# Row maxima of a 64 MB tensor: another split of the loads, and 48 blocks instead of 36 on GpSimd, 22 of them read out by a diagonal selection and summing copies

## The chip, the cores and the metric

The kernel runs on one core of a Trainium2 chip. The metric is the device time of one execution in microseconds (us), the median of several runs. One further execution is taken with the hardware profiler; its rows are what this document reads.

## What is computed

```python
x = np.random.randn(32, 512, 1024).astype(np.float32)
out = np.max(x, axis=-1)          # (32, 512), float32
```

16384 rows of 1024 numbers; each row gives its maximum. All 67.1 MB are read once from HBM.

## The kernel before

**Tiling.** The 16384 rows are laid over 128 partitions, 128 rows for each. A *load* of n rows brings n whole rows to every partition (n x 4 KB each, n x 512 KB in all) by one DMA on SyncE's (SP's) queue. `BLOCKS` lists the sizes: 17 loads, of 2, 16, 14, 15, 13, 12, 10, 9, 8, 7, 6, 4, 3, 2, 2, 1 and 1 rows, numbered from 0. The last three rows come in six *pieces* of 384 to 640 columns (`PIECES`: row, width). The data lands in `ring`, which has room for 47 rows a partition: loads take places in order and start again from the front when the next doesn't fit. A load is issued (`issue`, L263 to L276) when the program has passed the last reader of the place it overwrites; on the chip SP then waits for that reader's semaphore. Each of eight semaphores serves every eighth transfer, so a transfer also waits until the one eight before it has landed.

**VectorE** reduces whole rows: `direct` (L215, steps d) takes the rows of one load in one `reduce_max` (every reduction is recorded at L76, the helper `maximum`). For a piece (steps f) it reduces the piece together with one column in front of it, in which the maximum of the row's earlier piece lies.

**GpSimd's share.** `SHARED` maps a load to (rows, blocks of 128 columns of each such row, rows per chunk, ...): these blocks go another way, 36 of the 1024 in this kernel, in chunks of 3 or 6 blocks. For a chunk k:

- t: TensorE transposes its 128x128 blocks into PSUM (`turn`, L148; L155)
- c: ScalarE copies them to SBUF, tile `sb` (`fetch`, L162; L166)
- r: GpSimd takes the maximum over the 128 partitions, `partition_all_reduce`, into `top` (`across`, L169; L173); every partition then holds all the results
- b: TensorE turns row 0 of `top` back, one 1x128 transpose a block, into `small` (`back`, L177; L184)
- e: ScalarE copies these columns beside the rest of the row's partial maxima (`keep`, L192; L194)

The other columns of such rows are reduced by VectorE (`partial`, L221, steps p), and a last small reduction joins both (`merge`, L228, steps m). The loads in `RANK` write into one tile `joint` and share one merge, m99, at the very end; load 10 has tile `parts` and m10. `select` (L196, steps s) and `sums` (L204, steps x) are in the kernel's text, but its plan doesn't call them.

**Order.** `PLAN` (L30) writes out the order of all steps by hand; `in_turn` chains the instructions of each engine in that order, so every engine is one queue in which an instruction that waits holds up all behind it. The tiles `ps`, `sb` and `top` have two buffers each: chunk k waits until chunk k-2 has been read. The results of the first 116 rows a partition are stored behind the first f step, those of the last 12 after m99, both from ScalarE's queue (L301, L303).

Of the kernel before, what the change touches and what calls it, by code (L numbers as in the profile page):

```python
# [10 lines left out]


BLOCKS = [
    [2, 16, 14, 15, 13, 12, 10, 9, 8, 7, 6, 4],
    [3, 2, 2, 1, 1],
]
RING = 47

SHARED = {10: (6, 3, 2, 0), 12: (3, 3, 2, 0), 14: (2, 3, 1, 0), 16: (1, 3, 2, 0)}


RANK = {12: 1, 14: 2, 16: 2}


PIECES = [(2, 640), (0, 576), (1, 512), (1, 512), (0, 448), (2, 384)]


PLAN = """  # L30
    d0 d1 d2 d3 d4 d5 d6 d7 d8 d9 t0 p10 t1 c0 r0 t2 c1 d11 r1 c2 b0 e0 r2 b1 e1 t3 p12 t4
    c3 b2 c4 r3 d13 e2 r4 m10 t5 p14 b3 c5 t6 r5 d15 e3 b4 c6 t7 p16 e4 r6 b5 f0 c7 e5 f1 r7
    b6 f2 e6 f3 b7 f4 e7 f5 m99
""".split()

NOSYNC = mybir.DependencyInfo(mybir.DependencyClass.NoSync, mybir.DependencyReason.DATA)
# [4 lines left out]
def kernel(  # L41
# [33 lines left out]
    def maximum(out, in_):  # L75
        return in_turn("DVE", nc.vector.reduce_max(out=out, in_=in_, axis=X))  # L76
# [17 lines left out]
    views = []  # L94
    last = 1 + max(r for r, _ in PIECES)
    first = at = 0
    for sizes in BLOCKS:
# [6 lines left out]
        b, place = 0, {}  # L104
        for i in sorted(range(len(sizes)), key=lambda i: RANK.get(base + i, 0)):
            place[i] = b
# [8 lines left out]
    assert first == I  # L115
    shared = [SHARED.get(j, (0, C, 1, 0)) for j in range(len(loads))]

    lead = [n - s[0] for (_, n, _, _), s in zip(loads, shared)]
    final = [j for j in range(len(loads)) if j in RANK]
    final.sort(key=lambda j: loads[j][3])  # L120
# [10 lines left out]
    def rows(j):  # L131
        start, n, _, _ = loads[j]
        return ring[:, I + start * D:I + (start + n) * D].rearrange("p (i d) -> p i d", d=D)
# [5 lines left out]
    def share(j):  # L139
        m, parts, _, _ = shared[j]  # L140
        if j in RANK:
            r = loads[j][3] + lead[j] - col0
            return joint[:, r:r + m, :]
        if j not in fetched:
            fetched[j] = once.tile([P, m, parts + (parts < C)], F32, name=f"parts{j}")
        return fetched[j]
# [74 lines left out]
    def partial(j):  # L221
        m, parts = shared[j][:2]

        s = width - parts if j in RANK else 1
        maximum(share(j)[:, :, parts:], rows(j)[:, lead[j]:lead[j] + m, parts * P:].rearrange(
# [14 lines left out]
    before = [None] * last  # L240
    for r, w in PIECES:
        c, q = done[r], before[r]
# [90 lines left out]
```

## Time and profile before

| | |
|---|---|
| median of 3 runs | 163.65 us (163.60 to 163.66) |
| the profiled execution | 163.59 us, of it 161.8 us from the first to the last instruction (span) |
| mean DMA rate over the span | 415 GB/s (67.11 MB read) |
| VectorE (DVE) busy | 135.5 us, 84% of the span |
| GpSimd (POOL) busy | 15.9 us, 8 all-reduces from 141.3 us on |
| TensorE (PE) | 13.3 us; ScalarE (ACT) 7.3 us |

How to read it: a row of a group names the line, the engine, the operation, the tiles written and read, the count, and then the busy time, the mean duration of one in ns, and the idle time of the engine ahead of it with what ended it. Rows in order of time give the start and the length in us. SPq and ACTq are the queues of SP and ScalarE that issue DMAs. An instruction often starts some 0.08 to 0.1 us before the one ahead of it in its engine has ended, so durations add up to a little more than the time they take.

### The profile page before, as it was taken

What the parts mean: (1) busy time and instruction counts of PE and PEld (TensorE: products, weight loads), DVE (VectorE), ACT (ScalarE), POOL (GpSimd) and SP (SyncE); (2) the same over time, 40 slices, a digit from 0 to 9 for tenths busy, and PEclk for the clock granted to TensorE, in tenths of its full rate; (3) what the DMA queues carried; (4) which work ended last, traced back from release to release, by engine and by line L of the source; (5) the groups of instructions that cost most, each with busy time, mean ns of one, the idle gap of its engine ahead of it and who ended that gap; (6) DMA issues with size and microseconds to landing.
All of it is one profiled execution on the core that took longest, in us unless ns stands there. A gap on an engine that the chain in (4) does not pass through costs nothing.

```text
span 161.8 us, 304 instructions
## 1 busy us (share of the span) xinstructions
PE 13.3 (8%) x72; PEld 11.1 (7%) x72; DVE 135.5 (84%) x33; ACT 7.3 (5%) x17; POOL 15.9 (10%) x13
## 2 busy tenths in 40 slices
PE   0000000000000000000000000000000000647471
PEld 0000000000000000000000000000000000637350
DVE  3500009999999929999999999999999999999994
ACT  0020000000000000000000000000000000142230
POOL 0000000000000000000000000000000000097991
PEclk9999999999999999999999999999999999995555
DMA  5996998799999599999988997999999899999991
GB/s 198 579 486 292 518 472 383 312 454 454 486 486 486 243 454 421 421 448 561 401 389 389 486 466 344 437 437 421 478 429 439 376 475 395 433 410 412 408 389 38
DMA packets 3600, 67.18 MB, mean 415 GB/s; under 512 B 656, under 2 KB 912, under 8 KB 1680
## 3 DMA queue, kind: packets, MB, share of 16 engines
q1 hardware_dynamic: 3312, 67.11, 97.0%
q10 hardware_dynamic: 288, 0.07, 0.2%
HBM read 67.11 MB, written 0.07 MB: 415 GB/s over the span
## 4 chain that ended last, share of the span: by engine, by line
DVE 63%; DMA 35%; issue 0%; SPq 0%; DVEq 0%
DVE ring L76 58%; DMA ring<-in_x_dram 35%; DVE parts L76 3%; DVE joint L76 2%; SPq L270 0%; DVEq L328 0%; DVEq L76 0%
## 5 line engine op out<-in xcount | busy, mean ns | idle before, releaser
L76 DVE TENSOR_REDUCE ring<-ring 128x2 f32<-128x2048 f32 (+17 forms) x19 | 125.7, 6660 | 23.0 <-DMA ring<-in_x_dram 22.9
L173 POOL PARTITION_ALL_REDUCE top<-sb x8 | 15.6, 2013 | 134.9 <-ACT sb L166 134.5
L155 PE MATMUL ps<-ident,ring 128*128 128x128 f32 x36 | 8.9, 426 | 141.1 <-DMA ring<-in_x_dram 141.0
L155 PEld LDWEIGHTS ps<-ident,ring 128*128 128x128 f32 x36 | 7.0, 222 | 141.2 <-issue 141.2
L166 ACT COPY sb<-ps 128x768 f32<-128x768 f32 (+1 forms) x8 | 5.0, 640 | 139.1 <-PE ps L155 137.7
L184 PE MATMUL small<-ident,top 1*128 1x1 f32 x36 | 4.8, 238 | 4.4 <-POOL top L173 4.4
L184 PEld LDWEIGHTS small<-ident,top 1*128 1x128 f32 x36 | 4.1, 197 | 6.4 <-POOL top L173 5.0
L76 DVE TENSOR_REDUCE joint<-ring 128x3 f32<-128x1920 f32 (+2 forms) x3 | 4.4, 1483 | 0.0
L76 DVE TENSOR_REDUCE parts<-ring 128x6 f32<-128x3840 f32 x1 | 4.1, 4144 | 0.0
L166 ACT ACT_TABLE_LOAD x1 | 1.3, 1283 | 7.7 <-DVE ring L76 7.7
L194 ACT COPY joint<-small 128x3 f32<-128x3 f32 (+1 forms) x5 | 0.8, 164 | 2.3 <-PE small L184 2.3
L81 DVE MEMSET ident<- 128x128 f32 x1 | 0.2, 165 | 0.8 <-PEq L317 0.8
L288 POOL MEMSET gate<- 128x1 f32 x1 | 0.1, 100 | 7.3 <-DVE ring L76 7.3
L194 ACT COPY parts<-small 128x6 f32<-128x6 f32 x3 | 0.5, 166 | 2.6 <-PE small L184 2.5
L88 DVE TENSOR_SCALAR rowno<-rowno 32x1 f32<-32x1 f32 x3 | 0.4, 147 | 0.1
L83 DVE TENSOR_TENSOR_SCAN colno<-ident 128x128 f32<-128x128 f32 x1 | 0.4, 424 | 0.0
L90 DVE TENSOR_SCALAR ident<-colno,rowno 128x128 f32<-128x128 f32 x1 | 0.3, 286 | 0.0
L85 DVE STREAM_TRANSPOSE rowno<-colno 128x32 f32<-128x32 f32 x1 | 0.2, 211 | 0.0
L76 DVE TENSOR_REDUCE ring<-joint 128x6 f32<-128x24 f32 x1 | 0.2, 169 | 0.0
L76 DVE TENSOR_REDUCE ring<-parts 128x6 f32<-128x24 f32 x1 | 0.2, 168 | 0.0
L317 POOL MEMSET const-float32-0.0<- 128x1 f32 x1 | 0.1, 100 | 0.2 <-issue 0.2
L317 POOL MEMSET const-bfloat16-1.0<- 128x1 bf16 x1 | 0.1, 102 | 0.0
(3 smaller groups left out, 0.3 us busy)
## 6 DMA issues: line engine op xcount, KB each, us to landing
ring<-in_x_dram SPq DMA_DIRECT2D x1, 7680.0 KB, 57.6
ring<-in_x_dram SPq DMA_DIRECT2D x1, 7168.0 KB, 40.0
ring<-in_x_dram SPq DMA_DIRECT2D x1, 6656.0 KB, 33.6
ring<-in_x_dram SPq DMA_DIRECT2D x1, 6144.0 KB, 33.1
ring<-in_x_dram SPq DMA_DIRECT2D x1, 5120.0 KB, 26.2
ring<-in_x_dram SPq DMA_DIRECT2D x1, 4608.0 KB, 36.7
ring<-in_x_dram SPq DMA_DIRECT2D x1, 4096.0 KB, 32.9
ring<-in_x_dram SPq DMA_DIRECT2D x1, 3584.0 KB, 28.2
```

Of the source, the lines that this page charges most:

```text
L76: return in_turn("DVE", nc.vector.reduce_max(out=out, in_=in_, axis=X))
L81: in_turn("DVE", nc.vector.memset(ident, 1.0))
L83: in_turn("DVE", nc.vector.tensor_tensor_scan(out=colno, data0=ident, data1=ident, initial=-1.0, op0=ALU.add, op1=ALU.mult))
L85: in_turn("DVE", nc.vector.transpose(out=rowno, in_=colno[:, :32]))
L88: in_turn("DVE", nc.vector.tensor_scalar(out=part, in0=part, scalar1=float(q * 32), scalar2=None, op0=ALU.add))
L90: in_turn("DVE", nc.vector.tensor_scalar(out=ident, in0=colno, scalar1=rowno[:, 0:1], scalar2=None, op0=ALU.is_equal))
L155: in_turn("PE", nc.tensor.transpose(out=ps[:, w:w + P], in_=rows(j)[:, lead[j] + r + i, c * P:(c + 1) * P], identity=ident,))
L166: in_turn("ACT", nc.scalar.copy(out=sb[:, :W], in_=filled[k][:, :W]))
L173: in_turn("POOL", nc.gpsimd.partition_all_reduce(top[:, :W], turns[k][:, :W], P, bass_isa.ReduceOp.max))
L184: in_turn("PE", nc.tensor.transpose(out=small[:, i, c:c + 1], in_=tops[k][0:1, w:w + P], identity=ident[0:1, 0:1],))
L194: in_turn("ACT", nc.scalar.copy(out=share(j)[:, r:r + q, :shared[j][1]], in_=smalls[k]))
L317: nc = _bacc.Bacc("TRN2", target_bir_lowering=False, num_devices=1)
```

## The change

It changes the tables and the plan; the functions stay. The loads become 2, 15, 14, 16, 14, 13, 11, 10, 9, 7, 5, 3, 2, 2, 1, 1 and 1 rows, with four pieces for two rows. GpSimd's share grows to 48 blocks in ten chunks, from loads 8, 9, 10, 11, 13, 14 and 16; chunks have 6, 4, 6, 6, 8, 4, 6, 4, 2 and 2 blocks. Chunks 0 to 3 (22 blocks) are read out without TensorE: `select` on GpSimd sets to zero, in each 128x128 block of `top`, all but the diagonal, so that partition p keeps the maximum of row p, and `sums` on ScalarE adds up the 128 columns of each block with an accumulating copy, which leaves that maximum. The other chunks go through b and e as before. Four merges take the place of two: m8, m9, m10, m99.

```diff
 BLOCKS = [
-    [2, 16, 14, 15, 13, 12, 10, 9, 8, 7, 6, 4],
-    [3, 2, 2, 1, 1],
+    [2, 15, 14, 16, 14, 13, 11, 10, 9, 7, 5],
+    [3, 2, 2, 1, 1, 1],
 ]
-SHARED = {10: (6, 3, 2, 0), 12: (3, 3, 2, 0), 14: (2, 3, 1, 0), 16: (1, 3, 2, 0)}
-RANK = {12: 1, 14: 2, 16: 2}
-PIECES = [(2, 640), (0, 576), (1, 512), (1, 512), (0, 448), (2, 384)]
+SHARED = {8: (5, 2, 3, 1), 9: (4, 3, 2, 1), 10: (3, 4, 2, 0), 11: (3, 2, 4, 0), 13: (2, 2, 4, 0), 14: (1, 2, 1, 0), 16: (1, 2, 3, 0)}
+RANK = {11: 1, 13: 2, 14: 2, 16: 2}
+PIECES = [(0, 576), (1, 576), (0, 448), (1, 448)]
 PLAN = """
-    d0 d1 d2 d3 d4 d5 d6 d7 d8 d9 t0 p10 t1 c0 r0 t2 c1 d11 r1 c2 b0 e0 r2 b1 e1 t3 p12 t4
-    c3 b2 c4 r3 d13 e2 r4 m10 t5 p14 b3 c5 t6 r5 d15 e3 b4 c6 t7 p16 e4 r6 b5 f0 c7 e5 f1 r7
-    b6 f2 e6 f3 b7 f4 e7 f5 m99
+    d0 d1 d2 d3 d4 d5 d6 d7 t0 d8 t1 c0 c1 r0 p8 s0 r1 x0 s1 x1 t2 d9 t3 c2 r2 c3 m8 p9 s2
+    r3 x2 t4 d10 t5 c4 p10 s3 c5 r4 x3 t6 p11 m9 d12 r5 c6 b4 e4 r6 b5 p13 t7 e5 t8 c7 m10
+    p14 r7 c8 b6 d15 e6 p16 t9 r8 b7 c9 f0 e7 r9 b8 f1 e8 f2 b9 f3 e9 m99
 """.split()
```

The two functions that the plan newly calls (unchanged):

```python
def select(k):
    j, _, q = chunks[k]
    B = q * shared[j][1]
    view = tops[k][:, :B * P].rearrange("p (b w) -> p b w", w=P)
    in_turn("POOL", nc.gpsimd.affine_select(
        out=view, in_=view, pattern=[[0, B], [-1, P]], compare_op=ALU.is_equal,
        fill=0.0, base=0, channel_multiplier=1))

def sums(k):
    ...
    in_turn("ACT", nc.scalar.activation(
        out=tops[k][:, w:w + P], in_=tops[k][:, w:w + P],
        func=mybir.ActivationFunctionType.Copy,
        accum_out=share(j)[:, r + i, c:c + 1]))
```

## The prediction

> **What bounds the kernel now.** I read the slices first, then the stages (busy time, DMA share and GB/s in stretches that I set), then the chain of waits, then the tail in order of time. From the page:
>
> ```profile
> DMA  5996998799999599999988997999999899999991
> q1 hardware_dynamic: 3312, 67.11, 97.0%
> ```
>
> The dips of the DMA row are packets of 56 to 64 KB booked in the slice where they end; the stages even them out (us and length, PE, PEld, DVE, ACT, POOL busy, PE clock, DMA share, GB/s):
>
> ```profile
> 2.00:138.50 136.50, 0.00 (x0) 0.00 (x0) 113.52 (x13) 1.28 (x1) 0.10 (x1) 1.00 1.00 433
> 138.50:153.50 15.00, 9.50 (x52) 8.26 (x53) 15.00 (x7) 4.23 (x9) 11.23 (x5) 0.76 0.99 415
> 153.50:158.50 5.00, 3.49 (x21) 2.63 (x20) 4.93 (x8) 1.64 (x7) 4.40 (x4) 0.50 0.93 346
> ```
>
> From 2 us until about 158.5 the 16 DMA engines never rest. VectorE idles early (113.5 of 136.5 us busy) and is full only from 90 us. The chain of waits shows the one stretch of it that hides this:
>
> ```profile
> 56.91 33.10 DMA ring<-in_x_dram
> 90.00 0.02 issue
> 90.03 49.46 DVE ring L76 x5
> ```
>
> The chain puts 49 us on VectorE, but it starts when a load landed, and in the end VectorE only just keeps up with the loads: the last piece is issued at 153.44 us and takes 5.3 us to land, so 158.7, and its reduction starts at 158.87. In the order of time:
>
> ```profile
> 155.56 3.86 DVE L76 TENSOR_REDUCE ring<-ring 128x1 f32<-128x640 f32 x6
> 158.85 0.16 ACT L194 COPY joint<-small 128x3 f32<-128x3 f32 x1 [1.25 <-PE small L184]
> 159.33 0.17 DVE L76 TENSOR_REDUCE ring<-joint 128x6 f32<-128x24 f32 x1
> 159.53 0.34 ACTq L303 DMA_DIRECT2D out_dram<-ring  x1
> ```
>
> Two things meet at the final merge (m99, 159.33): the last piece's reduction, and GpSimd's last result, which lay ready at 159.02, 0.3 us early. **Both bounds count:** the load stream by a hair, GpSimd's chain close behind.
>
> **The load stream.** From the landings in the trace (5.32, 24.64, 41.58, 59.73, 75.47, 90.00, ... us) a load of n rows a partition costs 1.2045 n + 0.075 us; pieces cost 1.2045 us a row plus about 0.07 each (they land at 155.54, 156.30, 156.97, 157.65, 158.25, 158.72). The bytes stay, 17 loads stay 17, two pieces go: 2 x 0.07 = 0.14 us less. Laid out with the new sizes the landings are 105.7 (11 rows), 117.9 (10), 128.8 (9), 137.3 (7), 143.4 (5), 147.1 (3), 149.6, 152.05, 153.3, 154.6, 155.9, and pieces at 156.6, 157.4, 158.0, 158.57. The ring still gives room in time: load 4 (14) goes out when the 15 rows are reduced (39.6 us, with data queued until 59.7), load 8 (9) at 106.4 (queued until 117.9), load 10 (5) at 118.2 (queued until 137.3). SP's pieces wait only for the landing eight transfers earlier, the last for 149.6; it is needed at 158. So the stream does not stall.
>
> **VectorE.** A reduction costs 1.0415 ns an element plus 0.06 net (10.809 us for 10240, 4.419 for 4096, each starting 0.083 before the one ahead ends). It gives 12 more blocks away, 12 x 0.133 = 1.6 us, and gets 27 reductions for 24, +0.2: 1.4 us less work. None of it shortens the end, since it already waits for landings: laid row by row, it starts d9 at 137.3, d10 at 143.4, p13 at 152.06, p16 at 155.90, each as its load lands, and f3 (449 elements, 0.61 us, where the last was 385, 0.54) at 158.62; m99 follows at 159.15 and ends at 159.32. The same layout of the old plan gives 159.37 (the trace has 159.50). Difference: **-0.05 us**. Behind it nothing changes: the store's issue, its landing and the end take 2.3 us.
>
> **GpSimd.** Its rows:
>
> ```profile
> L173 POOL PARTITION_ALL_REDUCE top<-sb x4 | 10.0, 2543 | 134.5 <-ACT sb L166 134.5
> L173 POOL PARTITION_ALL_REDUCE top<-sb x4 | 5.7, 1483 | 0.4 <-PE small L184 0.4
> ```
>
> The first (140 to 150 us) are four of 768 columns, the second (from 152.3) four of 384. Back to back they start 2.486 and 1.407 us apart: 0.33 us + 2.81 ns a column, so 1.77 for 512, 3.21 for 1024, 1.05 for 256. The ten new ones sum to 20.5 us (15.6 before); the diagonal selections of 768, 512, 768 and 768 columns come on top, and no row shows one. **Bounds:** from below, GpSimd's memset of one element, 0.1 us; from above, the all-reduce of the same tile, 2.5 us, which also crosses partitions. The nearest row is an elementwise comparison, VectorE's is_equal on 128 columns, 0.286 us; at its 1.04 ns a column 768 would take 0.95. I take 1.0 us (0.7 for 512), on GpSimd an estimate.
>
> **The sums** are 22 small ScalarE passes with an accumulator, also in no row. ScalarE's copies: 800 ns for 768 columns and 479 for 384, so 0.16 + 0.00084 a column; 0.27 for 128, less the 0.10 by which neighbours overlap: 0.16 from below. From above, no overlap and a second small instruction (0.164): 0.43. I take 0.30. Gone are 22 of TensorE's 48 one-row transposes and four of ScalarE's small copies, both off the path; TensorE's 12 added transposes, 0.213 each, lie in its gaps (the largest group, t4, ends at 145.5, and c4 behind x2 starts at 145.57).
>
> Laid in the order written out: load 8 lands at 128.8; before, the first all-reduce began 2.7 us behind its landing (138.57 to 141.25), so r0 at 131.4, s0 133.98, r1 134.98, s1 136.8 to 137.5, sums x1 until 138.8. ScalarE's copy c2 stands behind x1 and needs load 9 (137.3 + 1.75): 139.05, so r2 starts at 139.9 and GpSimd rests 2.4 us. Then r2 2.5, s2 1.0, r3 2.5, s3 1.0 until 147.03; r4 needs c4, which stands behind x2 on ScalarE: ready 146.67, so 0.36 early. r4 to r9 then run without rest: 150.2, 151.9, 154.35, 156.1, 157.1 and, since r9 waits for the buffer of r7 to be read, 158.33. One transpose and one copy later, 159.0, its maxima are there; VectorE wants them at 159.15. Merges m8, m9 and m10 find their parts 1.7, 0.7 and 0.9 us early. **So the cover is about 0.15 us at the end, 0.3 with the pause before r9**, thinner than the trace's own 0.3; it is gone when a selection of 768 passes 1.2 us, or a sum 0.36.
>
> **Sum against the profiled 163.59:** 163.54; the median of the runs is 0.06 above it: **163.6 us**, no change. A measurement of this kernel can tell about 0.2% (0.33 us) from none.
>
> **Rivals.**
> A. *The selection is slow*, slower. GpSimd's only long row has 2.81 ns a column, so 1 ns is a hope. All four count, 3.3 times the excess, because s0 and s1 push c2 as s2 and s3 push r4: at 1.35 us +0.55, at 1.7 (midway of 0.95 and 2.5) +1.85, so 165.5; at 2.5, +4.8. It decides from 1.2 us. The Trainium skill's "GPSIMD Engine Reference" (3.1) speaks for it: even a tight one-input loop takes about 1.8 cycles an element at 1.2 GHz, two-input work 2.6; 768 columns would be estimated at 1.15 to 1.66 us, and the sum at 163.6 to 165.3. No run here shows which. Against A stands only that the other engines' elementwise rows lie near 1 ns a column.
> B. *The sums are slow and block ScalarE's queue*, slower: behind x2 wait c4 and so r4, behind x3 c6 and so r6. At 0.43 each +0.6 us, 164.2; with a selection of 1.35 as well, +1.6. For it: an accumulator that must be read out. Against: the 0.10 overlap in the rows.
> C. *VectorE is the bound*, faster, as the chain's 63% has it: the 1.4 us would count, 162.2. Against it: the DMA share of 1.00 and the reductions that start as loads land.
> That the change does not do what it says I rule out: the built order has 48 blocks, four selections, 22 sums and four pieces.
>
> **Chances.** Forecast 0.53; A 0.24 (mostly 1.3 to 1.8 us, 164 to 165.6); B 0.16 (164 to 165.2); C 0.07. So faster 0.07, same 0.53, slower 0.40. The forecast's own range is 163.4 to 163.9. The range runs to 165.4, which leaves out C and the dear third of A; the bounds of 2.5 and 0.43 together (+5.5, 169) lie beyond and hold some 0.04.
>
> **What would show it.** Right: the stages still show a DMA share of 1.00 until 158 us, the last piece is reduced near 158.6, m99 starts at once behind it, selections near 1.0 and sums near 0.30. A: selection rows over 1.2, m99 idle behind ScalarE's copy, no rest on GpSimd between s1 and r9. B: copies L166 idle-free behind L210, r4 waiting for ScalarE. C: the last piece landing before 157.5. I would be wrong altogether if a load were issued too late and the DMA share fell before 150 us.

## The result and the profile after

The changed kernel takes **164.09 us** (median of 9 runs, 164.00 to 164.38) against 163.66 (9 runs, 163.55 to 163.93): ratio 1.0026, 95% interval 1.0016 to 1.0037. It is slower by 0.43 us; 163.6 was forecast. The profiled execution, the slowest of the nine, took 164.38, of it 162.7 us span.

The page of the changed kernel, DMA row and queues (packets, MB, share of the 16 engines):

```profile
DMA  5999699999799979999999998989999899999990
...
q1 hardware_dynamic: 3024, 67.11, 96.4%
q10 hardware_dynamic: 288, 0.07, 0.2%
q14 instruction: 1, 0.01, 0.0%
```

The last row is new: one packet of instructions, 8 KB, while the kernel runs. The page of before has no such row. The stages, as in the prediction (PE, PEld, DVE, ACT, POOL busy, PE clock, DMA share, GB/s):

```profile
2.00:138.50 136.50, 3.15 (x14) 2.81 (x15) 112.05 (x14) 5.48 (x22) 5.86 (x5) 1.00 1.00 432
138.50:152.70 14.20, 7.33 (x41) 6.08 (x40) 14.20 (x9) 8.00 (x33) 12.33 (x7) 0.71 0.99 415
152.70:158.50 5.80, 3.80 (x20) 2.62 (x20) 5.58 (x7) 1.98 (x7) 5.17 (x4) 0.50 0.96 367
158.50:159.20 0.70, 0.12 (x1) 0.12 (x2) 0.70 (x2) 0.00 (x0) 0.53 (x1) 0.50 0.01 5
```

The DMA engines are as full as before, and the bytes are the same. VectorE is less busy than before (112.05 us for 113.52 until 138.5). The tail of VectorE in order of time:

```profile
152.38 1.76 DVE L76 TENSOR_REDUCE joint<-ring 128x2 f32<-128x1536 f32 x1
154.05 0.16 DVE L76 TENSOR_REDUCE ring<-parts 128x3 f32<-128x15 f32 x1
154.12 0.94 DVE L76 TENSOR_REDUCE joint<-ring 128x1 f32<-128x768 f32 x1
155.23 1.22 DVE L76 TENSOR_REDUCE ring<-ring 128x1 f32<-128x1024 f32 x1 [0.17 <-DMA ring<-in_x_dram]
156.51 0.95 DVE L76 TENSOR_REDUCE joint<-ring 128x1 f32<-128x768 f32 x1
157.38 2.46 DVE L76 TENSOR_REDUCE ring<-ring 128x1 f32<-128x576 f32 x4
159.76 0.17 DVE L76 TENSOR_REDUCE ring<-joint 128x7 f32<-128x21 f32 x1
```

m99 starts at 159.76 (before: 159.33), and VectorE waits for a load ahead of 155.23. The chain of waits ends in the loads as well:

```profile
129.07 0.02 issue
129.09 27.39 DMA ring<-in_x_dram
156.49 0.02 issue
156.51 0.95 DVE joint L76
```

So the stream of loads is late. A load is done when all 16 engines have landed their part. The trace's landings, first and last of the 16, in us:

```
                        changed            before           (one copy, below)
load 13, 2 rows      151.88  152.36                          151.81  152.19
load 14, 1 row       153.20  154.09     151.82  152.15 *     153.10  153.48
last piece           158.40  159.13     158.41  158.72       158.35  158.70
* load 14 of before has 2 rows and lies elsewhere in the stream
```

Between loads 13 and 14 the gap from first to last landing grows from 0.48 to 0.89 us, and it is still 0.72 at the end. With one copy it goes from 0.38 to 0.35 over the same loads, so some 0.27 us of the step is left at the last piece. At load 14 one engine lands 0.46 us behind the fifteenth. The first engine ends as early as before (158.40, 158.41); the load is done when the late one is. The packets of that time show why:

```
q14  8192 bytes  at 152.78 us, 313 ns
q1   4096 bytes  at 153.10 us, 319 ns     (usual: 160 ns)
q1   4096 bytes  at 153.40 us, 379 ns
```

A window around it has the packet in the profile's own view:

```profile
q1 hardware_dynamic: 63, 0.20, 102.7%
q14 instruction: 1, 0.01, 3.9%
```

It comes when ScalarE stands at its 63rd row of 81 (before has 34 rows in all). The profiled run of the changed kernel has slower packets of 56 to 64 KB at 11 to 47 us too; by load 13 it is 0.17 us behind the run with one copy (152.36, 152.19). Such packets come up in another profiled run (before_16_copies, below) whose median time is that of before, so they are taken as this run's own. And it loses 0.3 us behind m99: its last store is issued at 160.01 and lands at 161.78, after 1.77 us (before 1.41, with one copy 1.46). Of the 0.79 us between the two profiled executions only the 0.43 at m99 can so be put down to the loads; what the fetch costs in the median is read from the experiments.

### The profile page after: what moved, and what is told of

Same layout as the page of the kernel before. It is cut to its first block, busy times and chain, and to the rows that moved or that the text cites. A ratio compares the mean times of both kernels' runs of the same rounds, so it can differ in the third digit from the quotient of the medians.

```text
span 162.7 us, 367 instructions
## 1 busy us (share of the span) xinstructions
PE 14.6 (9%) x74; PEld 11.8 (7%) x74; DVE 134.3 (83%) x36; ACT 15.6 (10%) x61; POOL 24.1 (15%) x19
## 4 chain that ended last, share of the span: by engine, by line
DMA 77%; DVE 20%; SPq 0%; issue 0%; DVEq 0%
DMA ring<-in_x_dram 77%; DVE ring L76 19%; DVE joint L76 1%; SPq L270 0%; DVEq L328 0%
## 5 line engine op out<-in xcount | busy, mean ns | idle before, releaser
L76 DVE TENSOR_REDUCE ring<-ring 128x2 f32<-128x2048 f32 (+11 forms) x17 | 118.2, 6987 | 24.6 <-DMA ring<-in_x_dram 24.6
L173 POOL PARTITION_ALL_REDUCE top<-sb x10 | 20.6, 2093 | 127.1 <-ACT sb L166 126.4
L155 PE MATMUL ps<-ident,ring 128*128 128x128 f32 x48 | 11.3, 408 | 141.7 <-DMA ring<-in_x_dram 138.4
L155 PEld LDWEIGHTS ps<-ident,ring 128*128 128x128 f32 x48 | 8.7, 211 | 143.2 <-issue 133.6
L166 ACT COPY sb<-ps 128x768 f32<-128x768 f32 (+3 forms) x10 | 6.6, 669 | 127.1 <-PE ps L155 124.1
L76 DVE TENSOR_REDUCE parts<-ring 128x5 f32<-128x3840 f32 (+2 forms) x3 | 8.7, 2899 | 0.0
L210 ACT ACTIVATE top<-top 128x128 f32<-128x128 f32 x22 | 6.5, 296 | 6.0 <-POOL top L200 6.0
L76 DVE TENSOR_REDUCE joint<-ring 128x1 f32<-128x768 f32 (+2 forms) x4 | 6.2, 1549 | 0.1
L210 ACT ACTIVATION_READ_ACCUMULATOR top<-top 128x1 f32 x22 | 4.1, 186 | 0.0
L200 POOL TENSOR_SCALAR_AFFINE_SELECT top<-top 128x768 f32<-128x768 f32 (+1 forms) x4 | 3.2, 806 | 0.3
```

The lines of the kernel that those rows point to most:

```text
L155: in_turn("PE", nc.tensor.transpose(out=ps[:, w:w + P], in_=rows(j)[:, lead[j] + r + i, c * P:(c + 1) * P], identity=ident,))
L166: in_turn("ACT", nc.scalar.copy(out=sb[:, :W], in_=filled[k][:, :W]))
L173: in_turn("POOL", nc.gpsimd.partition_all_reduce(top[:, :W], turns[k][:, :W], P, bass_isa.ReduceOp.max))
L200: in_turn("POOL", nc.gpsimd.affine_select(out=view, in_=view, pattern=[[0, B], [-1, P]], compare_op=ALU.is_equal, fill=0.0, base=0, channe ...
L210: in_turn("ACT", nc.scalar.activation(out=tops[k][:, w:w + P], in_=tops[k][:, w:w + P], func=mybir.ActivationFunctionType.Copy, accum_out= ...
```

## The experiments

Theory F: the added ScalarE rows (22 accumulating passes are 44 rows, a pass and a read of the accumulator each) take ScalarE's queue past a block of instructions; fetching the next block takes one DMA engine out of a stream that never rests. Rivals: G, GpSimd's chain ends last; L, the new split of the loads is slower; R, ScalarE's added work at the end holds up what stands behind it. All are against runs of the kernel before on the same chip.

**1. after_one_copy.** In `sums`, one copy a chunk, which leaves the summing out (the removed lines are shortened here):

```diff
-        for i in range(q): for c in range(parts): nc.scalar.activation(..., accum_out=...)
+        in_turn("ACT", nc.scalar.copy(out=share(j)[:, r:r + q, :parts], in_=view[:, :, :, 0]))
```

> The changed kernel, but the 22 accumulating passes are replaced by four copies, one a chunk, that take column 0 of each block; what lands in the partial maxima of loads 8 and 9 is then not the row's maximum, so this kernel leaves the summing out. ScalarE has 4 rows in place of 44 there. Theory F (an 8 KB transfer of instructions on queue q14 at 152.8 us, seen only in the changed kernel, holds up one of the 16 DMA engines, and the last loads wait for that engine): the transfer is gone, the spread between the first and the last of a load's 16 landings stays near 0.3 to 0.5 us to the end (0.89 at load 14 in the changed kernel), and the time is 0.4 to 0.5 us below the changed kernel's 164.09, so 163.6 to 163.7. Rival G (GpSimd's chain is what ends last, since the final copy before m99 lay ready only 0.1 us early): GpSimd's rows are the same, the time stays within 0.15 us of 164.09. Rival L (the new split of the loads makes the stream slower, as packets of 56 to 64 KB took up to 0.28 us longer at 11 to 47 us): 164.09 stays as well, with the fetch gone.

Measured: 163.67 us; ratio to before 1.0000 (0.9991 to 1.0009). No q14 row, the spread 0.35 to 0.40 us from the first load to the last piece. GpSimd's ten all-reduces and four selections and the new loads are all there, so G and L as they were meant fall: with the fetch gone the slowdown is gone.

**2. before_44_copies, 3. before_16_copies.** To the kernel before, behind d0, in ScalarE's idle time:

```diff
+                for _ in range(44):        # 16 in the other
+                    in_turn("ACT", nc.scalar.copy(out=idle[:, 0:1], in_=ident[:, 0:1]))
```

> The kernel before with 44 copies of one column on ScalarE at about 8 us, where it has nothing to do for 130 us: as many more instructions on ScalarE as the sums brought (78 rows in place of 34). Theory F: ScalarE's queue now needs one more block of instructions, an 8 KB packet on q14 appears near the ScalarE row that is the 62nd (about 154 us), one engine falls behind by 0.4 us, and the time is 0.2 to 0.5 us above before (163.85 to 164.15). Rivals G and L: no difference, 163.66 within 0.1.

> The same with 16 copies, 50 rows on ScalarE. Theory F, if a count between 50 and 81 brings the transfer: no packet on q14 after the start, 163.66 within 0.1. If any added instruction cost time here (against F), it would lie between before and the run with 44.

Measured: 44 copies 164.01 us, ratio 1.0016 (1.0007 to 1.0025), with a q14 packet at 157.97; 16 copies 163.69, ratio 1.0000 (0.9991 to 1.0009), no packet. Work of 10 us in a hole of 130 us costs 0.3 us when it has enough rows, and nothing when it has not. But the profiled run with 44 copies, which took 163.86, less than the median, doesn't show F's path: the packet came too late to widen the spread of the last landings (0.54 at load 1, 0.45 at the last piece). It shows another delay. Behind its semaphore at 154.89 us ScalarE starts its 64th row, a copy, only 0.38 us later, where the same copy takes 0.06 us with 16 copies. GpSimd's last result then lies ready 0.07 us ahead of m99 (0.32 with 16 copies), and the last store goes out 0.28 us behind the start of m99 (0.20). So extra rows may also cost a pause of the engine itself; whether this pause belongs to the next block of instructions, and how much of the 0.3 us it makes, isn't shown. With 120 copies, below, rows 50 to 78 have no such pause.

**4. after_ten_sums.** Chunks 2 and 3 through steps b and e, and without s and x, in the plan.

> The changed kernel with chunks 2 and 3 read out by transposes and copies (steps b and e) as before, so 10 blocks instead of 22 go by selection and sums, two selections of 0.86 us and 24 rows of ScalarE less. The result is whole. Theory F: about 59 rows on ScalarE; if that stays under the count, no transfer in the middle and 163.55 to 163.7, below both kernels or level with before; if the transfer still comes, it comes later than 152.8 us and costs up to 0.4. Rival G: GpSimd has 1.7 us less to do, so 0.1 to 0.2 us less than 164.09 with or without the transfer. Rival L: 164.0 to 164.1.

Measured: 163.82 us, ratio to before 1.0010 (1.0001 to 1.0019): no q14 row with 58 rows on ScalarE, and the load stream ends at 158.66. Less than the changed kernel, as F has it, though 0.1 above what was expected and not better than before.

**5. before_120_copies, 6. after_60_more.** The same copies, 120 in the kernel before and 60 in the changed one, to bring the fetch forward.

> The kernel before with 120 copies of one column on ScalarE from 9 us on (0.22 us each, so until 36 us; ScalarE has nothing else before 140 us). Theory F, with a transfer of 8 KB of instructions each time ScalarE has gone through some 63 to 69 rows: a packet on q14 near 23 us, perhaps a second at the end. If the engine that carries it stays behind until the last load (the load queue never runs empty, so nothing lets it catch up), the time is 0.2 to 0.5 us above before as with the late transfer: 163.9 to 164.15. If it catches up, 163.7 within 0.1. Rival R (ScalarE's work at the end, not the transfer, cost the time in the changed kernel): no difference, 163.69.

> The changed kernel with 60 copies of one column on ScalarE from 9 to 23 us. Theory F: the transfer of 152.8 us comes at about 23 us instead, and no load of the end shows a new lag; the time stays at 164.0 to 164.2 if the lag is carried to the end, and falls to 163.6 to 163.7 if it is caught up or if only a late transfer costs. A second transfer at the end (141 rows in all) would add up to 0.4.

Measured (before: 163.90 on this chip): 164.26, ratio 1.0024 (1.0015 to 1.0033), packet at 24.13 us; 164.28, ratio 1.0025 (1.0016 to 1.0034), packet at 23.28 us, none at the end. The 1.0025 is the 1.0026 of the changed kernel. The fetch now falls 135 us from the end, and it costs as much: the late engine has hardly caught up. In after_60_more the spread is 0.41 us for the first load, 1.13 and 0.97 for the next two, 0.97 still at 158.31 and 0.89 at the last piece. The profile of the 120 copies can't show this. Its first load is already 0.75 us apart, before the copies begin, and the engine that carries the fetch is 0.63 us ahead of the slowest (their packets end at 24.13 and 24.76 us), which hides the 0.60 us that it loses; so this run's cost stands on its median alone.

R falls with the profile of the changed kernel: r4 starts at 147.06, with one copy, so without the sums, at 146.91, and these 0.15 us are what the loads are behind by then. GpSimd also rests 0.6 us before its last all-reduce, which waits for TensorE and so for load 16; a delay from the sums would have been taken up there.

```profile
POOL top L173 <- PE small L184: 0.6, 1, 0.6
```

**7. before_60_gpsimd, 8. before_60_vector.** 60 memsets of one element, on GpSimd in the same place, and on VectorE behind d0.

```diff
+                for _ in range(60):
+                    in_turn("POOL", nc.gpsimd.memset(gate[:, 1:2], 0.0))     # or "DVE", nc.vector.memset(idle[:, 0:1], 0.0)
```

> The kernel before with 60 memsets of one element on GpSimd at about 8 us (92 rows in place of 32), where it has nothing to do until 141 us. Theory F, if every engine fetches by its own count: a packet on q14 in the middle, +0.2 to +0.5 us. If the transfer belongs to ScalarE alone: no packet, 163.69 within 0.1.

> The same with 60 memsets of one element on VectorE behind its first reduction, in the 17 us in which it waits for the load of 16 rows (101 rows in place of 41). Theory F for every engine: a packet on q14, late, since VectorE's 62nd row then lies about 8 us in or, counted from the second block, near the end; +0.2 to +0.5 us. ScalarE alone: no packet, 163.69 within 0.1.

Measured: GpSimd 164.18, ratio 1.0019 (1.0010 to 1.0028), packet at 19.40 us, at GpSimd's 71st row; VectorE 164.60, ratio 1.0039 (1.0027 to 1.0052), packet at 17.08 us, at its 71st row. From the rows of the run with the memsets on VectorE, the memsets and then the page's queues:

```profile
L292 DVE MEMSET idle<- 128x1 f32 x60 | 3.5, 59 | 3.9
```

```profile
q1 hardware_dynamic: 3312, 67.11, 96.5%
q10 hardware_dynamic: 288, 0.07, 0.2%
q14 instruction: 1, 0.01, 0.0%
```

3.5 us of memsets in a wait of 17 us, and the kernel is 0.7 us longer. So each of the three engines fetches by its own count. What the carrying engine lost (fetch and excess in ns, their sum in us), and how the spread of the landings moved (us):

```
                    fetch   next packets' excess    sum     spread before, after
changed kernel        313   159 + 219              0.69     0.48 -> 0.89
after_60_more         309   293                    0.60     0.41 -> 0.97
before_60_gpsimd      309   254                    0.56     0.37 -> 0.77
before_60_vector      309   562                    0.87     0.34 -> 1.20
```

Where the carrier was not already the slowest of the 16, part of its loss is hidden. In the last three rows it was 0.11, 0.29 and 0.11 us ahead of the slowest when the fetch came, and the ends of the next packets spread 0.49, 0.27 and 0.76 us wider than those before: the sum less this lead. The landings spread by some 0.1 us more again, for which no run gives a cause.

**9. one_copy_select_twice, 10. ten_sums_smaller_end.** In the plan of the first experiment `s3 s3` for `s3`; in after_ten_sums `PIECES = [(0, 640), (1, 640), (0, 384), (1, 384)]`.

> The kernel with one copy a chunk instead of the sums (63.67 above 100, no transfer of instructions; what it leaves out is told there), with the last of the four selections done twice, which adds 0.86 us to GpSimd's chain and changes nothing in the data. If GpSimd's chain has the thin cover that the prediction gave it (0.15 us at the merge and 0.3 at the pause before r9), the merge comes 0.3 to 0.5 us later and the time is 0.3 to 0.5 us above the kernel before: 164.0 to 164.2. If GpSimd is hidden by more than that, no difference, within 0.1 of before. If every microsecond of GpSimd counts, +0.86.

> The changed kernel with ten sums (no transfer of instructions), with pieces of 640, 640, 384 and 384 columns for 576, 576, 448 and 448, so that the last reduction has 384 columns and one more: 0.07 us less behind the last landing. Nothing else changes. Theory F with a stream that is the only other bound: 0 to 0.1 us below after_ten_sums, level with the kernel before (within 0.2 us), and no version of this plan gains more, since the bytes are the same. If VectorE's 1.4 us of relief counted anywhere, it would show as 0.5 us or more below before.

(The "63.67 above 100" is 163.67.) Measured: 164.27, ratio to before 1.0039 (1.0025 to 1.0052), above the range expected; and 163.76, ratio 1.0006 (0.9997 to 1.0015). The end of the first, in order of time:

```profile
159.63 0.16 ACT L194 COPY joint<-small 128x2 f32<-128x2 f32 x1 [0.89 <-PE small L184]
159.69 0.38 ACTq L296 DMA_DIRECT2D out_dram<-ring  x1
159.83 0.17 DVE L76 TENSOR_REDUCE ring<-joint 128x7 f32<-128x21 f32 x1 [0.42 <-ACT joint L194]
160.17 0.39 ACTq L298 DMA_DIRECT2D out_dram<-ring  x1
```

and of the kernel with one selection less:

```profile
159.03 0.16 ACT L194 COPY joint<-small 128x2 f32<-128x2 f32 x1 [1.23 <-PE small L184]
159.10 0.38 ACTq L296 DMA_DIRECT2D out_dram<-ring  x1
159.33 0.16 DVE L76 TENSOR_REDUCE ring<-joint 128x7 f32<-128x21 f32 x1
159.57 0.39 ACTq L298 DMA_DIRECT2D out_dram<-ring  x1
```

The added selection moves r4 by 0.94 us (146.91 to 147.84) and m99 by 0.49: a cover of 0.45. The kernel with one selection less has it in two parts, a rest of 0.33 us before r9 and 0.14 at m99 (159.19 to 159.33). The prediction's sentence, "0.15 us at the end, 0.3 with the pause before r9", fits if the two are added; read as a total of 0.3 it was too thin. The store moves by another 0.1, which neither expected number had: the large store stands on ScalarE's queue behind e9, and the last store behind its 0.38 us of issue. As for the smaller end, it shows no gain that can be told from none, and with the load stream as the bound no version of this plan that was run beats the kernel before.

## Why the prediction failed, step by step

**What bounds the kernel: right.** The stream of loads to the end, GpSimd close behind. Rival C is out: in after_one_copy VectorE has its 12 blocks less, and the time is that of before.

**The load stream: the failed step.** "Laid out with the new sizes the landings are ... pieces at 156.6, 157.4, 158.0, 158.57 ... So the stream does not stall." The sizes were right: from the landing of the first load to that of the last piece it takes 153.24 us in after_one_copy and 153.40 before, 0.16 less where 0.14 was forecast. But the prediction looked for a stall only among loads issued late, and had no term for another transfer on the same engines. The changed kernel's last piece landed at 159.13. What the change brings to the stream is one fetch of instructions: 0.41 us in the landings of load 14, and a median 0.43 us longer, which is gone without the fetch. Fetches made by ScalarE at 23, 24 and 158 us go with ratios of 1.0025, 1.0024 and 1.0016, those by GpSimd and VectorE with 1.0019 and 1.0039.

**Behind m99: a smaller miss.** "Behind it nothing changes: the store's issue, its landing and the end take 2.3 us." From the start of m99 to the end of the span it is, with m99's own 0.17, 2.48 us before and 2.53 to 2.71 in the other runs of the changed plan, 2.91 in the profiled changed kernel. Part of it is the large store, which goes out later on ScalarE's queue (159.10 with one copy, 158.92 before) and holds up the last one by some 0.04 us; the rest is how long the last store takes to land, and why that varies (1.41 to 1.77 us) is open. With one copy the median is that of before all the same.

**The price of the sums: right in size, wrong in what was counted.** The rows of the changed kernel:

```profile
L210 ACT ACTIVATE top<-top 128x128 f32<-128x128 f32 x22 | 6.5, 296 | 6.0 <-POOL top L200 6.0
L210 ACT ACTIVATION_READ_ACCUMULATOR top<-top 128x1 f32 x22 | 4.1, 186 | 0.0
L200 POOL TENSOR_SCALAR_AFFINE_SELECT top<-top 128x768 f32<-128x768 f32 x3 | 2.6, 863 | 0.2
L200 POOL TENSOR_SCALAR_AFFINE_SELECT top<-top 128x512 f32<-128x512 f32 x1 | 0.6, 635 | 0.1
```

A sum starts 0.292 us behind the one ahead (0.30 was taken), as two overlapping rows; a selection of 768 takes 0.863 (1.0), of 512 0.635 (0.7). Each duration was near, and all were hidden as laid out. But their number is a cost of its own: 44 rows on ScalarE. The prediction had the rows' time and never counted them per engine.

**GpSimd's chain: right.** r2 started at 140.2 (forecast 139.9), r4 at 147.06 (147.03), and after_one_copy ends it at 158.58 (158.33), where m99 starts at 159.33 (159.15) with 0.14 us to spare; the later times go with a last piece that lands at 158.70 (158.57). Experiment 9 gives the cover. The count of reductions, "27 for 24", is 28 for 25 in the traces, the same difference. Rivals A and B did not come about, since the selection stayed under 1.2 and the sums under 0.36. By the Trainium skill's "GPSIMD Engine Reference" (3.1), as estimated in the prediction, 768 columns would take 1.15 to 1.66 us; the rows say 0.863.

**A rule beside it.** The Trainium skill, "Runtime: NRT & Kernel Launch" (Instruction fetch mechanics), has the sequencer fetch its next block of instructions through a DMA queue of its own, at a cost that is mostly hidden. The rows agree on the queue. They do not agree that the cost is hidden where the DMA engines are the bound: here it is 0.3 to 0.7 us for one block.

**What stays open.** At which instruction the fetch is made: it came at recorded rows 63 to 71 of its engine, and not in kernels with up to 58 rows on ScalarE; but the profile doesn't record all instructions, and TensorE runs 155 rows in the kernel before without a fetch in that time. Why 44 copies cost 0.3 us in the median when their profiled run shows no lag of a DMA engine but a pause on ScalarE. Why after_ten_sums, without a fetch, stays 0.13 us above before.

## What to carry to other kernels

Where the DMA engines are the bound from the first load to the last, count the instructions of each engine as well as their time: a few dozen tiny ones in an idle engine can bring one more fetch, and at 23 us it cost about what it cost at 153 us, since a late DMA engine has no time to catch up. Look for a q14 row on the page, and for the gap between the first and the last landing of a load. An accumulating pass on ScalarE counts as two rows.

## What was not expected of the hardware

One 8 KB fetch of instructions takes 0.31 us on one of 16 DMA engines, and the packets behind it there take 0.25 to 0.56 us more in all, so the engine loses 1.8 to 2.8 times what its own record shows. The 16 engines do not wait for each other between loads: in after_60_more and before_60_vector the spread was 0.97 and 1.20 us at load 2, and 0.89 and 1.11 us at the last piece, some 117 us later.
